# A two-layer transformer trunk on one core: where the weight casts, an activation table and the turned norm stand at the end of the attention heads

## The chip, the core and the metric

The kernel runs on one core of a Trainium2 chip. The metric is the device time of one execution in microseconds (us), the median of several runs; less is better. The core has four engines that matter here, each with its own queue of instructions worked in order: TensorE (PE, matrix products and transposes; PEld is its loading of the stationary operand), VectorE (DVE), ScalarE (ACT) and GpSimd (POOL). SyncE (SP) issues most of the DMAs. All data is float32; products are made in a split form, below.

## The reference

Two layers act on one sequence of 512 tokens with 1024 features. Layer 0 mixes tokens by attention, layer 1 by a gated spatial mixing, and each is followed by a dense MLP. What matters for this change is layer 0:

```python
h = rms_norm(x, norm_mix[i]) * (1.0 + sc1) + sh1
q, k, v = jnp.split(h @ w_in, 3, axis=-1)      # 16 heads of 64; q and k normed
s = q @ k.T + bias                             # per head, causal by chunks of 64
p = softmax(s)
y = (p @ v) @ w_out
x = x + g1 * y
h = rms_norm(x, norm_ffn[i]) * (1.0 + sc2) + sh2
x = x + g2 * (jnp.square(jax.nn.relu(h @ w1)) @ w2)   # w1: 1024 x 4096, w2: 4096 x 1024
```

## The kernel before

Tokens are tiled by 128 (four token tiles t), features by 128 (eight k). A float32 operand is split into a high part, rounded to the type that PE multiplies in one pass, and a low part, the rest. `mm3` makes three products (high x high, high x low, low x high) into one PSUM bank, so a token tile of 1024 features by 512 outputs takes 8 x 3 = 24 matmuls. Splitting a weight tile of 128 x 1024 takes one ScalarE cast (line L388 in `wload`, L485 in `Split`) and one VectorE subtraction (L389, L486). Buffers are 49 slots of one size that are handed out in turn: a new tile waits until the last reader of the slot's former tile is done, and the DMA that fills it waits in SP's queue.

The heads. A loop over heads has four parts in a pipeline: `head_a` (load the bias, turn q and k), `head_b` (scores, the addition of the bias with the row maximum on VectorE at L1218, the exponential on ScalarE at L1223), `head_c` (transposes of the probabilities, L1256, and their split, L1260 and L1261), `head_d` (product with v; then, for each pair of heads, the sums: copy L1284, add L1285, multiply L1293, and the split of the output into `oT` by L1300 and L1301). The output weights' left half is loaded in the loop (`out_load(0)`), and `out_early` makes the products of its first six k as PE has room, one token tile in each of the last turns of the loop.

Behind the loop PE's order is the program's (`in_order`); the order of the other engines, and that of PE inside the loop, is planned ahead of the run by a list scheduler with costs of its own, which takes instructions in the program's priority as soon as it counts them ready. `tc.issue_after(x)` adds the one rule that instructions of its block stay behind x on x's engine. What follows the loop: load x again, `out_load(1)` (right half of the output weights: four loads, four casts, four subtractions), the last `out_early`, the products of k = 6 for all token tiles, those of k = 7 (they need L1300 of the last pair) with the residual added for the left half (L424 multiplies by the gate, L425 adds), and then for each token tile the 24 products of the right half, the residual, and the norm in two steps:

- `norm.rows(t)`: two squares with row sums on ScalarE (L304), then on VectorE and ScalarE the inverse root (`rsqrt_m2`: L130, L131 with the activation Abs_reciprocal_sqrt, L133, L137), then VectorE scales the rows (L306).
- `norm.cols(t)`: PE turns the scaled rows by eight transposes (L315), ScalarE applies scale and shift (L319), VectorE splits (L325, L326).

In the kernel before, `norm.cols(t - 1)` stands behind the products of tile t, and that of the last tile stands in the MLP. `ffn` begins with eight up weights (`up_load` L740, `up_split`), four in each of two groups `ws[0]` and `ws[1]`; its first products take 256 tokens (tiles 0 and 1) at a time: the 96 of group 0, then `norm.cols(3)`, then the 96 of group 1, then the same for tiles 2 and 3. L844 stores x to DRAM.

Of the kernel before, what the change touches and what calls it, by code (L numbers as in the profile page):

```python
# [52 lines left out]
def trunk_kernel(  # L53
# [240 lines left out]
    def split_of(tiles):  # L294
        return [(tiles[k // 2][0][:, k % 2, :], tiles[k // 2][1][:, k % 2, :]) for k in range(2 * len(tiles))]

    normed = [None]

    def norm_rows(t, eng=V):
        nt, ni = SL.get([P, D], F32)  # L300
        ss = st.tile([P, 2], F32, tag="ss", name="ss")
        for hf in range(2):
            sl = slice(hf * 512, hf * 512 + 512)
            A.activation(nt[:, sl], xt[t][:, sl], AF.Square, scale=D ** -0.5, accum_out=ss[:, hf:hf + 1])  # L304
        r = rsqrt_m2(ss[:, 0:1], 1, 1, ss[:, 1:2])
        normed[0] = eng.tensor_scalar(nt, xt[t], r, -0.5, ALU.mult, ALU.mult)  # L306
        return nt, ni
# [441 lines left out]
    def up_ahead(l):  # L749
        return [up_split(up_load(l, 0, n)) for n in range(4)]  # L750

    def ffn(l, norm, rows, cols, after, bgn, lag=1):
        h = norm.h
        hid = {}
        y = Sum()
        xs = dp.tile([NT, P, D], F32, name=f"xs{l}")

        def up_part(w, ps, rng):
            for k in range(KD):
                mm3(ps, w.hi[:, k, :], w.lo[:, k, :], h[k][0][:, rng], h[k][1][:, rng], k == 0, k == KD - 1)  # L760

        def hid_new(b):
            hid[b] = [SL.get([P, 4, 256], F32) for _ in range(2)]

        def square_relu(ps, dsts):
            r = tp.tile([P, 512], F32, tag="tt", name="r")
            A.activation(r, ps, AF.Relu)  # L767
            n = 512 // len(dsts)
            for i, d in enumerate(dsts):
                v = r[:, i * n:i * n + n]  # L770
                if len(d.shape) == 3:
                    v = v.rearrange("p (a b) -> p a b", a=d.shape[1])
                A.activation(d, v, AF.Square)  # L773

        def up_done(b):
            if b == 7:
                norm.free()
            bg(bgn.pop(0) if bgn else 0)

        def up_steps(b):  # L780
            box = {}

            def load(n):
                box[n] = up_load(l, b, n)

            def prep(n):
                box[n] = up_split(box[n])

            def mult(n):
                if n == 0:  # L790
                    hid_new(b)
                w = box.pop(n)
                ps, pi = bank()
                up_part(w, ps, slice(0, 512))
                square_relu(ps, [hid[b][hf][0][:, n, :] for hf in range(2)])
                PS.free(pi)
                w.free()
                if n == 3:
                    up_done(b)

            return [Step(lambda n=n: load(n), lambda n=n: prep(n), nothing, lambda n=n: mult(n)) for n in range(4)]

        def quarters(q):
            return {(i, j): hid[2 * q + j][i] for i in range(2) for j in range(2)}

        def down_steps(q):
            steps = seven(Spent(lambda: quarters(q)), ffn_w2[l][q * 1024:(q + 1) * 1024, :], y)

            def mult_last(f=steps[-1].mult):
                f()  # L810
                bg(bgn.pop(0) if bgn else 0)

            steps[-1].mult = mult_last
            return steps

        ws = {0: ahead.pop("w") if ahead else up_ahead(l)}
        ws[1] = [up_split(up_load(l, 1, n)) for n in range(4)]
        steps = []
        for q in range(3):
            ups, downs = up_steps(2 * q + 2) + up_steps(2 * q + 3), down_steps(q)  # L820
            late = 2 if q == 2 else 1
            for i, u in enumerate(ups):
                steps += [u] + (downs[2 * (i - late):2 * (i - late) + 2] if i >= late else [])
            steps += downs[2 * (8 - late):]
        run = Run(steps, 4, 4)
        for hf in range(2):
            rng = slice(hf * 256, hf * 256 + 256)
            for b in range(2):
                if hf == 0:
                    hid_new(b)  # L830
                for j in range(2):
                    ps, pi = bank()
                    for n in range(2):
                        up_part(ws[b][2 * j + n], ps[:, n * 256:n * 256 + 256], rng)
                    square_relu(ps, [hid[b][hf][0][:, 2 * j:2 * j + 2, :]])
                    PS.free(pi)
                    if hf == 0 and b == 0 and j >= 2 - lag:
                        norm.cols(NT - 2 + j)
                if hf == 1:
                    for w in ws[b]:  # L840
                        w.free()
            if hf == 0:
                for t in range(NT):
                    SP.dma_start(xs[t], xt[t])  # L844
                    SL.free(xid[t])
        any_order()
        up_done(0)
        up_done(1)
        run.go()
        g = gbc[l, 5][0]  # L850
        in_order()
        parts = {b: Split(t, [P, 4, 256]) for b, (t, _) in quarters(3).items()}
        for b in (6, 7):
            SL.free(*[i for _, i in hid[b]])

        def spent(t):
            if t % 2:
                for j in range(2):
                    parts[t // 2, j].free()

        with tc.issue_after(mark[0].ins):
            merge = y.merge(xs, g)
            merge(0)
        project_last(plain(parts), ffn_w2[l][3072:4096, :], g, rows, cols, after, merge, spent)
# [331 lines left out]
        G.memset(b["bias"][0:64, 448:512], NEG)  # L1196
        hs[hd] = b

    rsums, rwide = {}, {}

    def head_b(hd):
        b = hs[hd]
        e = hd % 2
        q, ka, kb, ids = pairs[hd // 2]
        sc, i3 = SL.get([P, 2, 512], F32)
        b["ids"].append(i3)
        pt = {3: sc[:, 0, :], 2: sc[:, 1, 128:512], 0: sc[:, 1, 0:128], 1: b["bias"][:, 512:768]}
        nm = st.tile([P, NT], F32, tag="nm", name="nm")
        sm = st.tile([P, NT], F32, tag="sm", name="sm")
        if e == 0:  # L1210
            rsums[hd // 2] = st.tile([P, NT, 2], F32, tag="rs", name="rs")
        for it in range(NT):
            n = (it + 1) * P
            ps, pi = bank()
            cols = slice(it * P, it * P + P)
            mm(ps[:, 0:n], q[:, e, cols], ka[:, e, 0:n], True, False)
            mm(ps[:, 0:n], q[:, e, cols], kb[:, e, 0:n], False, True)
            V.tensor_tensor_reduce(  # L1218
                out=pt[it], in0=ps[:, 0:n], in1=b["bias"][:, 512 - n:512], scale=-1.0, scalar=-NEG,
                op0=ALU.add, op1=ALU.min, accum_out=nm[:, it:it + 1],  # L1220
            )
            PS.free(pi)
            A.activation(pt[it], pt[it], AF.Exp, bias=nm[:, it:it + 1], scale=-1.0, accum_out=sm[:, it:it + 1])  # L1223
        V.reciprocal(rsums[hd // 2][:, :, e], sm)
        if e == 1:
            SL.free(*ids)
            rb, rbi = rwide[hd // 2] = SL.get([P, 512], F32)
            G.tensor_copy(
                rb.rearrange("p (t e d) -> p t e d", t=NT, e=2),
                rsums.pop(hd // 2).unsqueeze(3).to_broadcast([P, NT, 2, HD]),  # L1230
            )
        b["pt"] = pt
# [34 lines left out]
    def head_d(hd):  # L1267
# [19 lines left out]
        if e == 1:  # L1287
            rp, ri = bank()
            rb, rbi = rwide.pop(pr)
            for t in range(NT):  # L1290
                T.transpose(rp[:, t * P:(t + 1) * P], rb[:, t * P:(t + 1) * P], ident)
            SL.free(rbi)
            V.tensor_tensor(sums[:, 1, :], sums[:, 1, :], rp, ALU.mult)  # L1293
            PS.free(ri)
            if pr % 2 == 0:
                tiles, ids = new_actT(2)
                oT["t"] += tiles
                oT["i"] += ids
            hi, lo = oT["t"][pr // 2]
            A.copy(hi[:, pr % 2, :], sums[:, 1, :])  # L1300
            V.tensor_tensor(lo[:, pr % 2, :], sums[:, 1, :], f32(hi[:, pr % 2, :]), ALU.subtract)  # L1301
            SL.free(si, vi)

# [88 lines left out]
    norm = mid = Norm(0, 3)  # L1392
    in_order()
    load_x()
    out_load(1)
    out_early(NT - 1)
    oTs = split_of(oT["t"])
    for t in range(NT):
# [6 lines left out]
    SL.free(*out_ids[0])  # L1405
    for t in range(NT):
        ps, pi = bank()
        gemm_tok(oTs, out_w[1], t, ps)
        add_residual(t, 512, ps, gbc[0, 2][0])
        PS.free(pi)  # L1410
        norm.rows(t)
        if t > 0:
            norm.cols(t - 1)
    SL.free(*out_ids[1])
    close(0, 2)
    for i, j in oT["i"]:
# [316 lines left out]
                kept.half(0)  # L1733

    lead[0], keep[0] = 2, 36
    ffn(0, mid, gate_rows, norm.cols, lambda: gate_load(0), [3] * 9)
    close(0, 5)
    xs = dp.tile([NT, P, D], F32, name="xsg")
    for t in range(NT):
# [78 lines left out]
```

## Time and profile before

| | |
|---|---|
| median of 3 runs | 1396.56 us (1395.19 to 1397.65) |
| profiled execution | 1395.72 us, its span 1393.7 us |
| PE busy | 1368.2 us (98%) |
| VectorE, ScalarE busy | 985.6 us (71%), 742.5 us (53%) |
| chain that ended last | PE 86%, VectorE 6%, DMA 4%, ScalarE 2% |
| mean granted clock of PE | 0.994 |

The span is what the profile covers; the execution's own time is about 2 us more. Times in the rows count from the span's start. In a timeline a line with xN is N instructions in a row, with the time from the start of the first to the end of the last; in brackets stands how long the engine was idle before it and whose result ended that.

### The profile page before, as it was taken

To read this page: it belongs to the slowest core of one execution; us is meant where nothing else is said; L and a number is where in the kernel's file an instruction comes from. 1 tells how busy PE (TensorE), PEld (TensorE's weight loads), DVE (VectorE), ACT (ScalarE), POOL (GpSimd) and SP (SyncE) were. 2 spreads that over 40 slices of the span, in tenths; PEclk is the share of its full clock that TensorE was granted. 3 is DMA by queue.
4 is the path that set the end of the run, shared out by engine and by line. 5 is a ranking of instruction groups with operands and counts; after the bars stand their busy time and mean duration, and the time that the engine had idled before them with its cause. 6 is when DMAs were issued, how large, how long until landed. Compare 5 with 4: busy or idle time off the path is not lost.

```text
span 1393.7 us, 18907 instructions
## 1 busy us (share of the span) xinstructions
PE 1368.2 (98%) x7130; PEld 1171.2 (84%) x7130; DVE 985.6 (71%) x1430; ACT 742.5 (53%) x1248; POOL 83.4 (6%) x98
## 2 busy tenths in 40 slices
PE   8999999899999999999999999999999999999998
PEld 7899888779888888888888888888889988888887
DVE  5888989675656776577797686778956455665672
ACT  6637667654554545446576654566435455554530
POOL 0000000000101101000000001000000010100100
PEclk8999999999999999999999999999999999999999
DMA  9747576564667875458445748575447366655541
GB/s 373 241 130 212 166 198 177 201 236 128 156 174 199 184 223 120 121 195 305 150 167 170 223 152 245 150 197 192 153 124 254 76 152 191 134 160 135 106 159 53
DMA packets 97483, 246.68 MB, mean 177 GB/s; under 512 B 8680, under 2 KB 10096, under 8 KB 97392
## 3 DMA queue, kind: packets, MB, share of 16 engines
q1 hardware_dynamic: 79536, 205.62, 44.4%
q0 software_dynamic: 16128, 33.56, 14.5%
q10 hardware_dynamic: 1728, 6.29, 1.2%
q8 instruction: 56, 0.92, 0.3%
q14 instruction: 35, 0.29, 0.1%
HBM read 219.23 MB, written 14.68 MB: 168 GB/s over the span
## 4 chain that ended last, share of the span: by engine, by line
PE 86%; DVE 6%; DMA 4%; ACT 2%; issue 1%; SPq 1%; DVEq 0%; ACTq 0%
PE p L92 83%; DMA s<-in_ada_w 1%; DMA s<-in_a_w_in 1%; DMA s<-xsg 1%; PE p L1623 1%; DVE s L979 1%; DMA s<-s 1%; PE p L1256 1%; ACT s L485 1%; SPq L1181 0%; DVE s L425 0%; PE p L315 0%; DMA s<-vd 0%; DVE s L1218 0%; DVE tr L424 0%
## 5 line engine op out<-in xcount | busy, mean ns | idle before, releaser
L92 PE MATMUL p<-s,s 128*128 128x512 f32 (+2 forms) x6496 | 1305.0, 361 | 10.9 <-DVE nm L1218 2.7
L92 PEld LDWEIGHTS p<-s,s 128*128 128x128 f32 x6496 | 1096.4, 189 | 193.7 <-DVE nm L1218 4.5
L486 DVE TENSOR_TENSOR s<-s,s 128x1024 fp32r<-128x1024 f32 x308 | 370.8, 1221 | 216.5 <-ACT s L485 157.9
L485 ACT CAST s<-s 128x1024 fp32r<-128x1024 f32 x308 | 316.9, 1050 | 199.7 <-PE p L92 110.4
L767 ACT ACTIVATE r<-p 128x512 f32<-128x512 f32 x64 | 38.2, 597 | 126.0 <-PE p L92 126.0
L194 DVE SCALAR_TENSOR_TENSOR s<-s,cs,s 128x1024 f32<-128x1024 f32 x70 | 89.6, 1280 | 14.6 <-DMA s<-in_ada_w 14.0
L627 POOL DMA_DIRECT2D s<-in_ffn_w x48 | 58.3, 1215 | 497.8 <-DVE s L486 392.2
L523 DVE TENSOR_TENSOR s<-s,p 128x512 f32<-128x512 f32 x76 | 50.2, 682 | 15.3 <-PE p L92 15.0
L388 ACT CAST s<-s 128x1024 fp32r<-128x1024 f32 x36 | 37.5, 1050 | 39.7 <-DMA s<-in_ffn_w 14.4
L389 DVE TENSOR_TENSOR s<-s,s 128x1024 fp32r<-128x1024 f32 x36 | 43.5, 1221 | 10.7 <-ACT s L388 10.5
L773 ACT ACTIVATE s<-r 128x256 f32<-128x256 f32 (+1 forms) x112 | 44.9, 442 | 1.4
L424 DVE TENSOR_TENSOR tr<-p,s 128x512 f32<-128x512 f32 (+1 forms) x33 | 22.0, 671 | 31.6 <-PE p L92 31.4
L536 DVE TENSOR_TENSOR s<-s,s 128x1024 f32<-128x1024 f32 x28 | 33.6, 1221 | 10.9 <-PE p L92 10.5
L1223 ACT ACTIVATE s<-s,nm 128x128 f32<-128x128 f32 (+3 forms) x64 | 36.0, 563 | 7.4 <-DVE nm L1218 6.0
L630 DVE TENSOR_TENSOR s<-s,s 128x1024 f32<-128x1024 f32 x28 | 33.9, 1220 | 5.6 <-DMA s<-in_b_w_in 5.4
L319 ACT ACTIVATE tt<-p,mod,mod 128x128 f32<-128x128 f32 x64 | 24.0, 462 | 21.1 <-PE p L315 10.4
L304 ACT ACTIVATE s<-s 128x512 f32<-128x512 f32 x24 | 15.3, 637 | 33.9 <-DVE s L425 32.8
L425 DVE TENSOR_TENSOR s<-s,tr 128x512 f32<-128x512 f32 (+1 forms) x33 | 22.2, 674 | 15.0 <-DMA s<-xsg 14.3
L1261 DVE TENSOR_TENSOR s<-p,s 128x512 fp32r<-128x512 f32 (+3 forms) x64 | 29.3, 484 | 4.0 <-ACT s L1260 3.7
L1218 DVE CUSTOM_DVE_ANT_0 s<-p,s 128x128 f32<-128x128 f32 (+3 forms) x64 | 29.6, 484 | 1.8 <-PE p L92 1.6
L1260 ACT CAST s<-p 128x512 fp32r<-128x512 f32 (+3 forms) x64 | 25.1, 425 | 7.5 <-PE p L1256 6.6
L1627 ACT COPY s<-p 128x512 f32<-128x512 f32 x24 | 13.8, 583 | 26.2 <-PE p L1623 26.2
(147 smaller groups left out, 769.5 us busy)
## 6 DMA issues: line engine op xcount, KB each, us to landing
s<-in_ffn_w SPq DMA_DIRECT2D x116, 512.0 KB, 4.2
s<-in_ada_w SPq DMA_DIRECT2D x96, 512.0 KB, 5.8
s<-in_ffn_w POOLq DMA_DIRECT2D x48, 512.0 KB, 5.8
s<-in_b_w_in SPq DMA_DIRECT2D x48, 512.0 KB, 4.7
s<-in_b_w_out SPq DMA_DIRECT2D x24, 512.0 KB, 4.5
s<-in_a_w_in SPq DMA_DIRECT2D x22, 512.0 KB, 4.7
s<-s SPq DMA_DIRECT2D x64, 128.0 KB, 3.5
vd<-s ACTq DMA_DIRECT2D x12, 512.0 KB, 3.8
```

What stands on the lines that cost most here:

```text
L92: T.matmul(ps, lhsT, rhs, start=start, stop=stop, skip_group_check=more)
L194: V.scalar_tensor_tensor(acc, r, ck, acc, ALU.mult, ALU.add)
L388: A.copy(hi, raw)
L389: engs[len(ids) // 2 % len(engs)].tensor_tensor(lo, raw, f32(hi), ALU.subtract)
L485: A.copy(self.hi, raw)
L486: mark[0] = V.tensor_tensor(self.lo, raw, f32(self.hi), ALU.subtract)
L523: V.tensor_tensor(dst, dst, ps, op)
L627: G.dma_start(raw[name, s_][0], block(i, j, s_), accum_op=ALU.add)
L630: V.tensor_tensor(raw[a, s_][0], raw[a, s_][0], raw[b, s_][0], ALU.add)
L767: A.activation(r, ps, AF.Relu)
L773: A.activation(d, v, AF.Square)
L1223: A.activation(pt[it], pt[it], AF.Exp, bias=nm[:, it:it + 1], scale=-1.0, accum_out=sm[:, it:it + 1])
```

## The change

Four edits, all around the end of the heads. The casts of the output weights' right half are kept behind the last exponential on ScalarE. A one-column Abs_reciprocal_sqrt of a constant is put behind the last output cast (L1300), so that the table which the norm needs is loaded there. The casts of the first four up weights are kept behind that same output cast, and those of the next four behind the last square of the norm. The norm's transposes of tile 0 and 1 are put inside the products of tile 2 (after four k) and tile 3 (after three k), and those of tile 2 and 3 behind the first and the second 48 up products (`lag` 2).

```diff
@@ norm_rows
-            A.activation(nt[:, sl], xt[t][:, sl], AF.Square, scale=D ** -0.5, accum_out=ss[:, hf:hf + 1])
+            squared[0] = A.activation(
+                nt[:, sl], xt[t][:, sl], AF.Square, scale=D ** -0.5, accum_out=ss[:, hf:hf + 1]
+            )
@@ ffn
-    def ffn(l, norm, rows, cols, after, bgn, lag=1):
+    def ffn(l, norm, rows, cols, after, bgn, lag=1, first=None):
...
-        ws = {0: ahead.pop("w") if ahead else up_ahead(l)}
-        ws[1] = [up_split(up_load(l, 1, n)) for n in range(4)]
+        with tc.issue_after(first.ins) if first is not None else nullcontext():
+            ws = {0: ahead.pop("w") if ahead else up_ahead(l)}
+        with tc.issue_after(squared[0].ins) if first is not None else nullcontext():
+            ws[1] = [up_split(up_load(l, 1, n)) for n in range(4)]
@@ head_b
-            A.activation(pt[it], pt[it], AF.Exp, bias=nm[:, it:it + 1], scale=-1.0, accum_out=sm[:, it:it + 1])
+            last_of["exp"] = A.activation(pt[it], pt[it], AF.Exp, bias=nm[:, it:it + 1], scale=-1.0, accum_out=sm[:, it:it + 1])
@@ head_d
-            A.copy(hi[:, pr % 2, :], sums[:, 1, :])
+            last_of["o"] = A.copy(hi[:, pr % 2, :], sums[:, 1, :])
@@ behind the heads
-    out_load(1)
+    with tc.issue_after(last_of["exp"].ins):
+        out_load(1)
+    u = st.tile([P, 1], F32, tag="ry1", name="ry")
+    with tc.issue_after(last_of["o"].ins):
+        A.activation(u, f32(ones)[:, 0:1], AF.Abs_reciprocal_sqrt)
...
-        gemm_tok(oTs, out_w[1], t, ps)
+        n = 6 - t if t > 1 else 4
+        gemm_tok(oTs, out_w[1][:n], t, ps, 0, KD - 1)
+        if t > 1:
+            norm.cols(t - 2)
+        gemm_tok(oTs, out_w[1][n:], t, ps, n, KD - 1)
         add_residual(t, 512, ps, gbc[0, 2][0])
         PS.free(pi)
         norm.rows(t)
-        if t > 0:
-            norm.cols(t - 1)
...
-    ffn(0, mid, gate_rows, norm.cols, lambda: gate_load(0), [3] * 9)
+    ffn(0, mid, gate_rows, norm.cols, lambda: gate_load(0), [3] * 9, 2, last_of["o"])
```

## Rows read from the trace of the kernel before

**Rows 1.** Page, busy time, share of the span and instructions of each engine.
```profile
PE 1368.2 (98%) x7130; PEld 1171.2 (84%) x7130; DVE 985.6 (71%) x1430; ACT 742.5 (53%) x1248; POOL 83.4 (6%) x98
```
**Rows 2.** PE's waits, 240 to 310 us: us in total, times, longest.
```profile
PE p L315 <- DVE s L306: 2.4, 2, 1.4
PE p L92 <- ACT s L1300: 2.1, 1, 2.1
PE p L1256 <- ACT s L1223: 1.8, 2, 1.6
PE p L92 <- DVE s L1261: 0.4, 2, 0.3
```
**Rows 3.** Stretches: length, busy time (instructions) per engine, PE's clock, DMA share, GB/s.
```profile
258.00:275.50 17.50, 15.26 (x76) 12.55 (x76) 11.56 (x18) 9.66 (x15) 0.62 (x1) 1.00 0.52 168
...
291.00:306.00 15.00, 13.55 (x72) 11.19 (x71) 12.02 (x31) 8.92 (x25) 0.00 (x0) 1.00 0.45 164
306.00:318.30 12.30, 12.30 (x107) 12.30 (x105) 5.58 (x14) 6.28 (x16) 0.00 (x0) 1.00 1.01 376
...
600.00:784.00 184.00, 184.00 (x833) 152.62 (x832) 138.10 (x148) 111.03 (x198) 4.78 (x6) 1.00 0.61 202
```
**Rows 4.** Timeline of the last exponential, 254 to 258 us.
```profile
253.52 0.68 DVE L1218 CUSTOM_DVE_ANT_0 s<-p,s 128x512 f32<-128x512 f32 x1
...
255.47 1.05 ACT L388 CAST s<-s 128x1024 fp32r<-128x1024 f32 x1 [0.37 <-DMA s<-in_a_w_out]
...
257.06 0.73 ACT L1223 ACTIVATE s<-s,nm 128x512 f32<-128x512 f32 x1
```
**Rows 5.** Timeline of the last pair's output, 270.9 to 277.7 us.
```profile
270.20 1.05 ACT L485 CAST s<-s 128x1024 fp32r<-128x1024 f32 x1 [3.10 <-DMA s<-in_ffn_w]
...
271.27 0.58 ACT L1284 COPY s<-p 64x512 f32<-64x512 f32 x1
271.28 1.23 DVE L486 TENSOR_TENSOR s<-s,s 128x1024 fp32r<-128x1024 f32 x1 [2.23 <-ACT s L485]
...
272.54 0.69 DVE L1285 TENSOR_TENSOR s<-p,s 64x512 f32<-64x512 f32 x1
273.27 0.69 DVE L1293 TENSOR_TENSOR s<-s,p 128x512 f32<-128x512 f32 x1
273.91 1.04 ACT L485 CAST s<-s 128x1024 fp32r<-128x1024 f32 x1 [2.06 <-DMA s<-in_ffn_w]
274.86 0.61 ACT L1300 CAST s<-s 128x512 fp32r<-128x512 f32 x1
```
**Rows 6.** Timeline of the first tile's norm, 286.9 to 291 us.
```profile
286.33 0.69 DVE L425 TENSOR_TENSOR s<-s,tr 128x512 f32<-128x512 f32 x1
...
287.80 1.28 ACT L131 ACT_TABLE_LOAD   x1
...
289.78 0.75 DVE L306 TENSOR_SCALAR s<-s,ru 128x1024 f32<-128x1024 f32 x1
```
**Rows 7.** Timeline of PE alone, 238 to 345 us.
```profile
275.53 14.16 PE L92 MATMUL p<-s,s 128*128 128x512 f32 x60 [2.10 <-ACT s L1300]
...
305.11 1.03 PE L315 MATMUL p<-ident,s 128*128 128x128 f32 x8
305.89 11.76 PE L92 MATMUL p<-s,s 128*128 128x256 f32 x96
```
**Rows 8.** Waits in SP's queue, 225 to 330 us: total, times, longest.
```profile
SPq L844 <- DVE s L425: 15.4, 3, 7.0
```
**Rows 9.** Line L740, the up weights' loads of 250 to 345 us.
```profile
DMA to landing us min/median/max: 3.6/5.4/12.6
```
**Rows 10.** Waits of PE's weight loads, 240 to 310 us: total, times, longest.
```profile
PEld p L92 <- ACT s L1300: 2.5, 1, 2.5
...
PEld p L315 <- DVE s L306: 1.9, 1, 1.9
PEld p L315 <- issue: 1.4, 1, 1.4
```

## What I expect, worked out before the change was run

> **What bounds the kernel now.** I read the busy times first: TensorE (PE) is busy for 1368.2 of 1393.7 us [rows 1], so only about 25 us of the span are PE idle, and a change that issues the same products can win no more than the part of that idle time which it touches. Next I read PE's waits by stretch. From 306 to 784 us the stretches show PE busy for every microsecond (12.30 of 12.30, 184.00 of 184.00, and two between [rows 3]); whatever is won before 306 us should therefore arrive at the end undiminished, unless the change makes a new wait there. The stretch that the diff touches, 258 to 306 us, has holes: 15.26 of 17.50 us busy in its first part, 13.55 of 15.00 in its last [rows 3]. The waits of 240 to 310 us name them [rows 2]: 1.6 us for the last exponential (L1223), 2.1 us for the last output cast (L1300), 2.4 us in two pieces for the scaled rows of the norm (L306), and up to 0.3 us for a subtraction (L1261). The granted clock is 1.00 in all these stretches [rows 3], so no time is to be had from it.
>
> **Output weight casts behind the last exponential.** The scores of the last 512-wide piece leave VectorE at 253.52 + 0.68 = 254.2 us; the exponential starts only at 257.06, because the weight cast of 255.47 (1.05 us, itself waiting 0.37 us for its DMA) and two casts of transposed rows stand ahead of it [rows 4]. Moving four casts away removes the weight cast from that place, and the exponential ends about 1.5 to 2 us sooner, before PE wants it. Gain 1.6 us, and 0.2 us for the subtraction wait behind it that hangs on the same casts; bounds 0 (the casts of transposed rows or a planned order take the place) to 1.9. The weights themselves are wanted only behind the twelve products that start at 275.53 (14.16 / 60 = 0.236 us each [rows 7]), so at 278.4, over 20 us behind the cast of 255.47; this slack hides the move, and without it each cast of 1.05 us would be PE's wait.
>
> **Up weight casts behind the last output cast.** The last pair of heads leaves PE and then runs through ScalarE 0.58, VectorE 0.69 and 0.69, ScalarE 0.61 us before PE may go on. Up weight work stands in between at each step [rows 5]: the copy starts at 271.27 when a cast (270.20 + 1.05) is over, the add starts at 272.54 after a 1.23 us subtraction of weights, and L1300, whose input is ready at 273.27 + 0.69 = 273.96, starts at 274.86 behind the cast of 273.91. Without these three the chain is 0.58 + 0.69 + 0.69 + 0.61 plus three hand-overs of about 0.05 = 2.7 us. PE covers it with the twelve products of the pair before (k = 6), 12 x 0.236 = 2.8 us. Nearly all of the 2.1 us goes; I leave 0.3 for hand-overs. Gain 1.8, bounds 0.9 (L1300's own delay alone, 274.86 - 273.96) to 2.1.
> What comes late instead: four casts (4.2 us) and their subtractions (4.9 us) now fall into the residual adds. Let S be the start of the products after L1300. VectorE then has 0.69 + eight adds of 0.68 + 4 x 1.22 = 11.0 us of work, ready at S + 11.0 where the first half of the second output pass is ready at S + 36 x 0.236 = S + 8.5: 2.5 us of delay for the first norm. That would cost PE in the old order; the next part hides it.
>
> **Norm turned two tiles behind.** From the residual add at 286.33 to the end of the scaled rows at 289.78 + 0.75 takes 4.2 us [rows 6], with one multiply of 0.68 before: 4.9, or 3.6 without the table load. Before, PE wanted those rows at the end of the second tile, S + 60 x 0.236 = S + 14.2; now it wants them twelve products later, S + 17.0. They come at S + 8.5 + 3.6 = S + 12.1, or S + 14.6 with VectorE's delay: at least 2.4 us to spare. The second tile's rows come at S + 14.2 + 3.6 = S + 17.8 and are wanted after eight transposes (0.8 us, 305.11 to 305.89 [rows 7]), twelve and nine products, S + 22.8: 5 us to spare. So both pieces of 2.4 us go; bounds 1.4 (one piece stays) to 2.4. The first up products now follow the second tile's transposes by only 15 products, 3.5 us, and read its eight columns one after the other; if ScalarE and VectorE serve the third tile's residual first, a part of a microsecond is lost there. I take 0.4, bounds 0 to 1.0. The third tile is turned after the first 48 up products; this moves 0.8 us of transposes and costs nothing.
>
> **Table asked for ahead.** The load of 1.28 us stood in the first norm's chain [rows 6]; behind L1300 it stands ahead of four casts that nobody wants for 27 us. With the two-tile distance the norm is no longer PE's wait, so I cost this edit at 0; without that distance it would be worth up to 1.3.
>
> **Second group of up weights behind the last square.** The last token tile ends on PE at S + 22.8 + 0.8 + 3.5 = S + 27.1; add 1.4 and square 0.8 give S + 29.3, four casts S + 33.5, the last subtraction S + 34.7. Their products start after 96 products (11.8 us, [rows 7]) and two sets of transposes at S + 40.5. Cost 0, cover 6 us and more.
>
> **Sum.** 1.6 + 0.2 + 1.8 + 2.4 - 0.4 = 5.6 us. The profiled execution took 1395.72 (span 1393.7 and 2.0 around it), so 1390.1; the median of the three runs stands 0.84 above it, so I forecast 1391.0. With each term's near and far bound the gain is 0 + 0.9 + 1.4 - 1.0 = 1.3 to 1.9 + 2.1 + 2.4 = 6.4. A difference under 0.2%, 2.8 us, can hardly be told from none.
>
> **Rivals.** *The head end gives nothing.* The four output weight casts (4.2 us on ScalarE, 4.9 on VectorE) now lie between the last exponential and the last pair's transposes, each still behind its DMA, and hold up the casts of the last probabilities as they held the exponential; the planned order on PE may shift as well. Then the first two gains stay away and 2.4 us of L306 are left: 1394.1. For it speaks that one weight cast that waited sufficed to cost 1.6 us; against it that PE has two groups of 18 early output products (18 x 0.236 = 4.2 us each) over this place and one full chain less of weights in it. [...]
> *The holes are wider than PE's rows say.* The weight loads have waits of their own in the same places, 2.5, 1.9 and 1.4 us [rows 10], 5.8 together where the products wait 2.1 + 2.4 = 4.5. If this start-up is regained too, the sum before deductions is 6.0 + 1.3 = 7.3 us: 1389.3. Against it: a weight load that waits while products ahead of it still run has lost nothing. [...]
> *Slower: the second group of up weights comes late.* The third and fourth load of that group reuse buffers that PE lets go in the last token tile, and SP works in order behind the stores of x, which held it for up to 7.0 us [rows 8]. Issued behind the last store, at about S + 29.7, and with cast and subtraction (2.3 us) they must have landed by S + 44.0 for the third tile's product at S + 46.3: a flight of 14.3 us. The slowest of before took 12.6 [rows 9], in the stretch where the DMA share was 1.01 [rows 3], and loads that reuse the four raw buffers held longer now join that stretch. From 14.3 us on PE waits; above 19.9 the whole gain is gone. With twice 12.6 PE waits 10.9: 1391.0 + 10.9 = 1401.9.
> *No effect*: the plan for the other engines comes out differently and puts as much idle time elsewhere: 1396.6.
>
> **How the numbers follow.** Forecast 0.63 (own range 1389.6 to 1393.0), wider holes 0.10, head end gives nothing 0.17, no effect 0.05, slower 0.05. Faster by over 0.2%: the first two, 0.73; within: 0.22; slower: 0.05. The range runs from 1388.6, just below the wider holes, to 1395.6, above the head-end rival; outside are the last two rivals and a tail.
>
> **What would show it.** In the profile after: no PE wait of L1256 for the last exponential; the wait for the last output cast at 0.5 us or less, with S near 272; no wait of the norm's transposes (L315 of before) for scaled rows; the table load near 273; the first 256-wide up products near 299 instead of 305.89; PE still busy throughout to 780. It is wrong if transposes of the first tile wait inside the third tile's products, if up products wait for a weight cast, or if the last pair's chain again starts behind weight work.

## The result

The changed kernel ran at a median of 1389.64 us (1387.55 to 1390.47, 4 runs), the kernel before beside it at 1397.11; the ratio is 0.9950, 95% interval 0.9932 to 0.9967, so 4.6 to 9.5 us less. With more runs (the first experiment below) it is 0.9970 (0.9959 to 0.9981), 2.7 to 5.7 us less. The forecast of 1391.0, 5.6 us less, lies in both, in the second just inside its edge. The profiled execution took 1389.62 us, its span is 1387.8.

First the waits of PE, 240 to 320 us (us in total, times, longest). Lines of the changed kernel have moved: L1223 is now L1227, L1261 L1265, L1285 L1289, L1300 L1304, L306 L308, L315 L317, L389 L391.

```profile
PE p L92 <- DVE s L1265: 0.7, 1, 0.7
PE p L1260 <- DVE s L1289: 0.4, 1, 0.4
PE p L1295 <- DVE s L1265: 0.4, 1, 0.4
PE p L92 <- DVE nm L1222: 0.2, 1, 0.2
```

Against [rows 2] the three large waits are gone: none for the exponential, none for the last output cast, none of the transposes for scaled rows. Three new ones stand there, 1.5 us together, for subtractions and an addition on VectorE. PE's own timeline shows where:

```profile
240.33 4.88 PE L92 MATMUL p<-s,s 128*128 128x512 f32 x22 [0.18 <-DVE nm L1222]
...
254.70 4.35 PE L92 MATMUL p<-s,s 128*128 128x512 f32 x18
...
260.14 0.33 PE L1260 MATMUL p<-ident,s 128*128 128x128 f32 x1 [0.44 <-DVE s L1289]
260.82 0.63 PE L1295 MATMUL p<-ident,s 128*128 128x128 f32 x4 [0.35 <-DVE s L1265]
262.20 26.52 PE L92 MATMUL p<-s,s 128*128 128x512 f32 x118 [0.75 <-DVE s L1265]
288.56 1.04 PE L317 MATMUL p<-ident,s 128*128 128x128 f32 x8
...
312.04 33.23 PE L92 MATMUL p<-s,s 128*128 128x256 f32 x275
```

Three marks of this view serve for all that follows: the 22 products ahead of the last exponentials (here 240.33), the long run of products behind the last head's transposes (262.20; before 263.78), and the first product of the second up group (312.04; before 318.28). From the first mark to the second it took 21.9 us before and takes 21.9 us now: the 1.6 us that PE no longer waits for the exponential come back as the three waits. From the second to the third it took 54.5 and takes 49.8. The whole stretch shrank from 76.4 to 71.7, by 4.7 us. Behind it both kernels have the same way to go (1075.4 and 1075.8 us to the end of the span). The rest of the difference of the two spans, 1.5 us, lies ahead of any edit: the 22 products start at 241.85 before and at 240.33 after. A longer fall of PE's clock in the first 40 us (from 15 to 30 us it was 0.65 to 0.69 before, 0.73 to 0.95 after) had set the kernel before back by 1.65 us, but that was made up by 171 us, where the same transposes start at 170.85 and 170.76. The lead comes from a second fall, in before and not in after, between 188 and 194 us (0.50 from 190 to 192 us, where after has 1.00); the stretch (length, busy time of the engines, clock, DMA share, GB/s) of before and of after:

```profile
186.00:194.00 8.00, 6.43 (x29) 5.59 (x30) 8.00 (x24) 5.50 (x14) 0.00 (x0) 0.79 0.72 206
```

```profile
186.00:194.00 8.00, 6.55 (x44) 5.89 (x44) 8.00 (x26) 5.51 (x13) 0.00 (x0) 1.00 0.76 209
```

PE is busy about as long in both, and does 29 instructions in the one and 44 in the other; behind it the lead is 1.9 us (the next transposes start at 193.62 and 191.74).

So of the 5.9 us between the two spans only some 4.4 belong to the change (4.7 won, 0.3 lost behind the stretch).

### The profile page after: what moved, and what is told of

Same layout as the page of the kernel before. It is cut to its first block, busy times and chain, and to the rows that moved or that the text cites. A ratio compares the mean times of both kernels' runs of the same rounds, so it can differ in the third digit from the quotient of the medians.

```text
span 1387.8 us, 18908 instructions
## 1 busy us (share of the span) xinstructions
PE 1365.1 (98%) x7130; PEld 1168.0 (84%) x7130; DVE 985.6 (71%) x1430; ACT 742.3 (53%) x1249; POOL 83.5 (6%) x98
## 3 DMA queue, kind: packets, MB, share of 16 engines
q0 software_dynamic: 16128, 33.56, 14.6%
## 4 chain that ended last, share of the span: by engine, by line
PE 86%; DVE 6%; DMA 4%; issue 2%; ACT 2%; SPq 0%; POOL 0%; DVEq 0%; ACTq 0%; POOLq 0%
PE p L92 83%; DMA s<-in_a_w_in 1%; DMA s<-xsg 1%; DMA s<-in_ada_w 1%; PE p L1633 1%; DVE s L1222 1%; DVE s L1265 0%; PE p L1260 0%; DMA s<-vd 0%; ACT s L487 0%; DMA s<-s 0%; PE p L207 0%; PE p L317 0%; DVE s L427 0%; DVE s L194 0%
## 5 line engine op out<-in xcount | busy, mean ns | idle before, releaser
L391 DVE TENSOR_TENSOR s<-s,s 128x1024 fp32r<-128x1024 f32 x36 | 43.4, 1222 | 10.3 <-ACT s L390 10.1
L426 DVE TENSOR_TENSOR tr<-p,s 128x512 f32<-128x512 f32 (+1 forms) x33 | 22.0, 672 | 31.6 <-PE p L92 31.3
L1227 ACT ACTIVATE s<-s,nm 128x128 f32<-128x128 f32 (+3 forms) x64 | 36.0, 564 | 7.8 <-DVE nm L1222 6.4
L427 DVE TENSOR_TENSOR s<-s,tr 128x512 f32<-128x512 f32 (+1 forms) x33 | 22.1, 675 | 15.0 <-DMA s<-xsg 14.4
L1265 DVE TENSOR_TENSOR s<-p,s 128x512 fp32r<-128x512 f32 (+3 forms) x64 | 29.3, 486 | 2.8 <-ACT s L1264 2.4
L1264 ACT CAST s<-p 128x512 fp32r<-128x512 f32 (+3 forms) x64 | 25.0, 427 | 5.5 <-PE p L1260 4.4
```

The costliest lines, as they stand in the source:

```text
L391: engs[len(ids) // 2 % len(engs)].tensor_tensor(lo, raw, f32(hi), ALU.subtract)
L1227: last_of["exp"] = A.activation(pt[it], pt[it], AF.Exp, bias=nm[:, it:it + 1], scale=-1.0, accum_out=sm[:, it:it + 1])
```

## The experiments

All are compared with the kernel before, run beside them on the same chip. "Stretch" is the time from the first to the third mark in the one profiled execution of each; in the first profile of the changed kernel it was 71.7.

| run | ratio to before (95% interval) | stretch, us |
|---|---|---|
| kernel before | 1 | 76.4 |
| e1 changed kernel | 0.9970 (0.9959 to 0.9981) | 72.5 |
| e2 output casts free | 0.9969 (0.9958 to 0.9979) | 71.8 |
| e3 norm one tile behind | 1.0004 (0.9993 to 1.0014) | 77.1 |
| e4 up casts free | 0.9969 (0.9958 to 0.9981) | 72.6 |
| e5 norm's edit alone | 0.9986 (0.9975 to 0.9998) | 73.7 |
| e6 no early table | 0.9976 (0.9965 to 0.9987) | 74.0 |
| e7 output casts behind the probabilities | 0.9944 (0.9932 to 0.9957) | 69.3 |
| e8 output casts behind the output | 0.9973 (0.9961 to 0.9984) | 73.4 |
| e9 as e7, again | 0.9942 (0.9927 to 0.9957) | 69.3 |
| e10 as e7, up casts free | 0.9988 (0.9978 to 0.9998) | 74.2 |
| e11 as e7, no early table | 0.9954 (0.9939 to 0.9968) | 69.3 |

**e1, the changed kernel.** No edit.

> The changed kernel itself, as the measure for the next runs. Compared is also the stretch on PE from the 22 products ahead of the last exponentials to the first product of the second up group: 318.28 - 241.85 = 76.4 us before, 312.04 - 240.33 = 71.7 in the changed kernel. Theory A (the gain is all in this stretch, 2.1 at the last output cast and 2.4 at the norm, while the 1.8 at the last exponential are given back right behind it): stretch 71.7 within 0.3, time 4 to 5 us below the kernel before. Theory B (a further 2 to 3 us are gained elsewhere, as the medians of 1389.64 and 1397.11 would have it): the same stretch, time 7 us below.

1391.53 us beside 1395.04 before. The ratio gives 4.2 us less and leaves little room for theory B's 7; the stretch came out at 72.5, 0.5 more than theory A's bound, through another 0.24 us wait for a subtraction and small shifts in the heads. The 7.5 us between the first medians were a small sample (4 runs each).

**e2, output casts free.**

```diff
-    with tc.issue_after(last_of["exp"].ins):
-        out_load(1)
+    out_load(1)
```

> The changed kernel without the first edit: the output weight casts are free to stand ahead of the last exponential again. Theory A (edit worth nothing, its four subtractions on VectorE only move the wait to the transposes and products behind): stretch 71.5 to 72.5 us, time within 1 us of the changed kernel; the wait of 1.6 us for the exponential is back and the waits for the subtractions of the last head's probabilities (1.5 us together) are gone. Theory B (edit worth its 1.8 us as forecast): stretch 73.5, time 1.8 us above the changed kernel.

1391.76 us, as e1. PE's waits, 238 to 325 us:

```profile
PE p L1260 <- ACT s L1227: 1.6, 2, 1.3
PE p L92 <- DVE s L1265: 0.7, 3, 0.3
...
PE p L92 <- DVE s L328: 0.2, 1, 0.2
```

The wait for the exponential is back (1.3) and the new waits are gone, apart from small ones that the kernel before has too; the wait for L328 belongs to the norm's edit (the deduction, below). The edit is worth nothing where it was put. VectorE in the changed kernel shows why:

```profile
255.40 2.36 DVE L391 TENSOR_TENSOR s<-s,s 128x1024 fp32r<-128x1024 f32 x2 [0.76 <-ACT s L390]
...
258.14 1.22 DVE L391 TENSOR_TENSOR s<-s,s 128x1024 fp32r<-128x1024 f32 x1
259.39 0.69 DVE L1289 TENSOR_TENSOR s<-p,s 64x512 f32<-64x512 f32 x1
260.12 0.56 DVE L1265 TENSOR_TENSOR s<-p,s 128x384 fp32r<-128x384 f32 x1
260.59 1.22 DVE L391 TENSOR_TENSOR s<-s,s 128x1024 fp32r<-128x1024 f32 x1
261.72 0.42 DVE L1265 TENSOR_TENSOR s<-p,s 128x256 fp32r<-128x256 f32 x1
```

The casts follow the exponential at once, and their four subtractions (L391, 1.2 us each) stand between the short subtractions and the addition for which PE waits: L1289 is wanted by the transposes of 260.14 and L1265 by those of 260.82 and the products of 262.20.

**e3, the norm's transposes one tile behind again.**

```diff
-        n = 6 - t if t > 1 else 4
-        gemm_tok(oTs, out_w[1][:n], t, ps, 0, KD - 1)
-        if t > 1:
-            norm.cols(t - 2)
-        gemm_tok(oTs, out_w[1][n:], t, ps, n, KD - 1)
+        gemm_tok(oTs, out_w[1], t, ps)
...
+        if t > 0:
+            norm.cols(t - 1)
...
-    ffn(0, mid, gate_rows, norm.cols, lambda: gate_load(0), [3] * 9, 2, last_of["o"])
+    ffn(0, mid, gate_rows, norm.cols, lambda: gate_load(0), [3] * 9, 1, last_of["o"])
```

> The changed kernel with the norm's transposes back at one tile behind, as before; the table still asked for ahead, the casts still held back. Theory A (the distance of two tiles is what hides the norm): two waits of the transposes for the scaled rows, 2 to 3.5 us together, time 2 to 3.5 us above the changed kernel. Rival (the early table alone would have taken the first wait away): one wait of about 1.4 us at the second tile, none at the first.

1396.15 us, 4.6 above e1: all of the gain is gone. There is one wait, not two, and at the first tile, not the second, so neither theory had it quite: the early table did not save the first transposes, since the up weights' casts and subtractions now stand in the residual adds. PE's wait and what followed, from the timeline and the stretches:

```profile
290.52 1.75 PE L317 MATMUL p<-ident,s 128*128 128x128 f32 x8 [2.12 <-DVE s L308]
291.92 6.75 PE L92 MATMUL p<-s,s 128*128 128x512 f32 x24
298.51 1.03 PE L317 MATMUL p<-ident,s 128*128 128x128 f32 x8
299.30 5.73 PE L92 MATMUL p<-s,s 128*128 128x512 f32 x24
```

```profile
290.52:292.00 1.48, 1.48 (x9) 1.48 (x9) 0.45 (x1) 1.48 (x3) 0.00 (x0) 0.57 0.15 58
292.00:294.00 2.00, 2.00 (x7) 1.61 (x6) 1.23 (x5) 2.00 (x8) 0.00 (x0) 0.50 0.54 219
```

The hole of 2.1 us is followed by transposes and products at 0.57 and 0.50 of the full clock. Eight transposes take 1.75 us where the next eight take 1.03, 24 products 6.75 where the next 24 take 5.73: another 1.7 us on top of the wait. Another 1.6 us of this profile's stretch are not the edit's: the clock fell as well behind the three short waits near 262 us, which this kernel has in common with the changed one (0.57 between 263 and 267 us). So the edit's own price in the profile is 2.1 + 1.7 = 3.8 us.

**e4, up casts free.** The two `issue_after` in `ffn` taken away.

```diff
-        with tc.issue_after(first.ins) if first is not None else nullcontext():
-            ws = {0: ahead.pop("w") if ahead else up_ahead(l)}
-        with tc.issue_after(squared[0].ins) if first is not None else nullcontext():
-            ws[1] = [up_split(up_load(l, 1, n)) for n in range(4)]
+        ws = {0: ahead.pop("w") if ahead else up_ahead(l)}
+        ws[1] = [up_split(up_load(l, 1, n)) for n in range(4)]
```

> The changed kernel with the up weight casts free. Theory A (these casts and subtractions in the last pair's chain cost the 2.1 us of the last output cast): that wait is back at 1.5 to 2.1 us, time 1.5 to 2.1 us above the changed kernel. Rival (with the heads' order changed PE no longer waits there anyway): wait under 0.5 us, time the same within 0.5.

1391.34 us, the same as e1 in time; in the profile the wait for the last output cast (here L1302) is back at 1.3 us:

```profile
PE p L92 <- ACT s L1302: 1.3, 1, 1.3
```

In time this run does not decide between the two answers: the interval of each ratio is about 1.5 us to either side. In the profile the 1.3 us do not come through whole either: from the second mark to the third it takes 0.9 us longer than in the changed kernel (50.77 and 49.84), since 0.4 us that are lost there further on, at the up products (the deduction, below), are not lost here. e10 asks again.

**e5, the norm's edit alone** on the kernel before.

```diff
-        gemm_tok(oTs, out_w[1], t, ps)
+        n = 6 - t if t > 1 else 4
+        gemm_tok(oTs, out_w[1][:n], t, ps, 0, KD - 1)
+        if t > 1:
+            norm.cols(t - 2)
+        gemm_tok(oTs, out_w[1][n:], t, ps, n, KD - 1)
...
-        if t > 0:
-            norm.cols(t - 1)
...
-    ffn(0, mid, gate_rows, norm.cols, lambda: gate_load(0), [3] * 9)
+    ffn(0, mid, gate_rows, norm.cols, lambda: gate_load(0), [3] * 9, 2)
```

> The kernel before with the norm's edit alone (transposes two tiles behind, lag 2); all casts free, no early table. Theory A (the edits add up: 2.4 at the norm, 2.1 at the last output cast): the two waits for the scaled rows are gone, the waits of 1.6 for the exponential and 2.1 for the output cast stay; stretch on PE from the 22 products to the second up group 74.0 us, time 2.4 us below the kernel before. Rival (the norm's edit carries all of it, since the run with the up casts free was as fast in time as the changed kernel): 4 us below.

1393.32 us; the ratio gives 2.0 us less (0.3 to 3.5), the stretch 73.7 where 74.0 was expected. The transposes no longer wait; the other two waits stay:

```profile
PE p L92 <- ACT s L1300: 2.7, 1, 2.7
PE p L1256 <- ACT s L1223: 1.3, 2, 1.1
```

The edits add up (theory A): 2 to 2.7 us are the norm's.

**e6, no early table.**

```diff
-    u = st.tile([P, 1], F32, tag="ry1", name="ry")
-    with tc.issue_after(last_of["o"].ins):
-        A.activation(u, f32(ones)[:, 0:1], AF.Abs_reciprocal_sqrt)
```

> The changed kernel without the early table: the load of 1.28 us stands again in the first tile's norm. Theory A (the first norm has 2.4 us or more to spare under the distance of two tiles): no wait of the transposes, stretch 71.7 within 0.3, time the same within 0.5. Rival (the early table is what keeps the first transposes on time): a wait of up to 1.3 us at the first transposes.

1392.78 us, 0.6 in a thousand above e1, inside both intervals. The transposes do not wait. The stretch is 74.0 all the same, and the reason that the profile shows is not the table: after the waits near 262 us the clock fell.

```profile
259.00:264.00 5.00, 3.33 (x19) 2.40 (x18) 4.94 (x8) 3.28 (x7) 0.00 (x0) 1.00 0.37 108
264.00:268.00 4.00, 4.00 (x11) 3.12 (x11) 1.74 (x4) 0.62 (x1) 0.00 (x0) 0.57 0.26 49
```

PE was busy for 3.33 of 5.00 us, and then ran eleven products in 4 us, where the same 4 us hold 21 in e1, at a clock of 1.00. The 118 products took 28.17 us where e1's and the changed kernel's took 26.5: 1.6 us. The same waits stand in the profiles of the changed kernel, e1, e3, e4 and e6; in e3 and e6 the clock fell behind them, to 0.57; in the changed kernel and e1 it stayed at 1.00, and e4's 46 products behind them were as fast as e5's without them (9.65 and 9.67 us).

**e7, output casts behind the last head's probabilities.** The first edit with another instruction to stay behind: the last cast of `head_c` (L1264).

```diff
-            A.copy(dst[:, 0, :], src)
+            last_of["p"] = A.copy(dst[:, 0, :], src)
...
-    with tc.issue_after(last_of["exp"].ins):
+    with tc.issue_after(last_of["p"].ins):
         out_load(1)
```

> The changed kernel with the output weight casts held back further, behind the last cast of the last head's probabilities instead of the last exponential. Theory A (the four subtractions ahead of the last probabilities' own caused the 1.5 us of new waits): neither the wait for the exponential nor those for the probabilities' subtractions; from the 22 products to the 46 behind the heads 20.2 us instead of 21.9, time 1.5 us below the changed kernel. Rival (the same work then stands in the last pair's chain): wait for the last output cast 1 us or more, time as the changed kernel.

1387.60 us (1386.05 to 1389.59), the fastest: 7.8 us below the kernel before (6.0 to 9.5). Its waits on PE in 236 to 325 us, and PE's three marks:

```profile
PE p L92 <- DVE s L1265: 0.3, 1, 0.3
PE p L1260 <- ACT s L1227: 0.2, 1, 0.2
PE p L92 <- DVE nm L1222: 0.2, 1, 0.2
```

```profile
239.44 4.86 PE L92 MATMUL p<-s,s 128*128 128x512 f32 x22 [0.20 <-DVE nm L1222]
...
259.10 26.29 PE L92 MATMUL p<-s,s 128*128 128x512 f32 x118
...
308.71 7.55 PE L92 MATMUL p<-s,s 128*128 128x256 f32 x61
```

From the first mark to the second it takes 19.7 us instead of 21.9, 0.5 less than expected. On VectorE the four weight subtractions now stand behind the last L1265, in a place where PE has products queued:

```profile
259.45 0.89 DVE L1265 TENSOR_TENSOR s<-p,s 128x512 fp32r<-128x512 f32 x2 [0.23 <-ACT s L1264]
260.56 4.63 DVE L391 TENSOR_TENSOR s<-s,s 128x1024 fp32r<-128x1024 f32 x4 [0.23 <-ACT s L390]
```

In time the step from e1 is 3.6 us, in the stretch 2.4 to 3.2. That the rest is the clock fits the profiles, since no wait above 0.3 us is left here, but is not shown.

**e8, output casts behind the last output cast.** As e7 with `last_of["o"]`.

> The changed kernel with the output weight casts behind the last output cast, beside the first up weights. Theory A (nothing in the heads needs them): no new wait in the heads, 20.2 us from the 22 products to the 46, and the right half's products, which start 2.8 us after the output cast, just get their first weights (cast 1.05 and subtraction 1.22 us, plus the table's 1.28 if that stands ahead); time 0.5 to 1.5 us below the changed kernel. Rival (the weights come too late): the right half's products wait for casts and subtractions, 1 to 4 us, time 0 to 3 us above the changed kernel.

1392.10 us, as e1. The heads are as quick as in e7 (19.7 us between the first two marks), and the right half's products wait only 0.4 us for a subtraction. What neither theory named: eight casts and eight subtractions now stand in the residual adds, and the first norm is late.

```profile
PE p L317 <- DVE ru L137: 2.0, 1, 2.0
PE p L92 <- DVE s L391: 0.4, 1, 0.4
```

```profile
287.10:289.10 2.00, 0.03 (x1) 0.00 (x0) 1.54 (x7) 0.80 (x4) 0.00 (x0) 1.00 1.01 403
289.10:293.00 3.90, 3.85 (x14) 3.36 (x15) 3.16 (x7) 3.68 (x9) 0.00 (x0) 0.56 0.15 59
```

Here too the clock fell behind a hole of 2.0 us, to 0.56.

**e9, e7 again**, beside the last two.

> The version with the output weight casts behind the last head's probabilities once more, as the measure for the two runs beside it and as a repeat on another occasion. Theory A: 69.3 us within 0.3 on PE from the 22 products to the second up group, time 7 us (5.5 to 8.5) below the kernel before. Rival (its lead over the changed kernel was luck of the occasion): 4 us below.

1387.66 us beside 1396.43; stretch 69.3. The lead is no luck of the occasion.

**e10, e7 with the up casts free** (the diff of e4).

> That version with the up weight casts free. Theory A (they cost the last pair's chain 1 to 2 us on PE, and the equal time of the earlier run with free casts was the resolution of the timing and 0.8 us of other waits in the profile beside it): a wait of 1.2 to 2.7 us for the last output cast, stretch 70.5 to 72, time 1 to 2.5 us above the run beside it. Rival (holding them back is worth nothing, since what is won at the output cast is paid later): time the same within 0.5.

1394.62 us, 6.4 above e9 by the ratios. PE's wait for the last output cast, ScalarE ahead of it, and PE's stretch behind it:

```profile
PE p L92 <- ACT s L1302: 3.6, 1, 3.6
```

```profile
271.81 1.05 ACT L487 CAST s<-s 128x1024 fp32r<-128x1024 f32 x1 [1.74 <-DMA s<-in_ffn_w]
272.76 0.61 ACT L1302 CAST s<-s 128x512 fp32r<-128x512 f32 x1
```

```profile
273.43:277.00 3.57, 3.57 (x9) 2.57 (x10) 3.03 (x4) 3.33 (x4) 0.00 (x0) 0.54 0.85 286
```

On ScalarE the output cast stands behind an up cast that waits 1.74 us for its DMA and takes 1.05. The wait is a microsecond longer than theory A's bound: the heads are done 2 us sooner than in e4, but PE's products go on at 273.43 here and at 273.21 there, since the same weights are waited for. Behind the wait the clock falls, to 0.54: the 72 products that follow take 18.29 us, and in e5 16.88 (16.89 in e4, whose clock is 1.00 from 273.2 to 279 us), so 1.4 us more. Once the heads are free, holding the up casts back is worth more in time than any other edit measured here.

**e11, e7 without the early table** (the diff of e6).

> That version without the early table. Theory A (worth nothing under the distance of two tiles): no wait of the first transposes, time the same within 1 us. Rival (the table's 1.28 us delay the first norm past its 2.4 us to spare): a wait of 0.1 to 1 us at the first transposes and 1 us in time.

1389.05 us, stretch 69.3, no wait of the transposes. The ratio lies 1.2 in a thousand (1.7 us) above e9's, and the intervals overlap; the profile shows no microsecond of it in the stretch. Far behind it this profile loses 3.3 us against e9's between 686 and 825 us, at a wait that the two kernels without the early table show (1.7 us in e6), and of the others e10 alone, at 0.3:

```profile
PE p L92 <- ACT s L1609: 2.0, 1, 2.0
```

A subtraction of weights on VectorE waits for a store to DRAM that sets its buffer free, 2.6 us here, 2.3 in e6 and not at all in e9, and the inverse root of layer 1 stands behind it. Whether that hangs on the missing table or on the spread of the store is open; both profiled executions are the slowest of their kernels. At the place it was made for, the table is worth nothing that can be shown; what it is worth over the whole, 0 to 1.7 us, these runs do not tell.

## Why the prediction was right, and where it was not

**The sum.** 5.6 us forecast, 4.7 in the profiled stretch, 4.2 (2.7 to 5.7) by the larger sample. The first term was not there, the second came out above its size, the third as forecast, and the deduction was paid: 2.1 + 2.4 - 0.4 = 4.1. The other 0.6 us of the 4.7 had no term: the holes gave back somewhat more than PE's waits (below). That the total lies near the forecast is in part luck: a term of 1.8 us was missing, and the first four runs of the changed kernel (7.5 us between the medians) flattered it.

**Output weight casts behind the last exponential: 1.8 forecast, 0 measured.** This is the step that failed. It looked at ScalarE alone, where the weight cast did stand ahead of the exponential. It priced the four subtractions that follow the casts (4.9 us of VectorE) only in the rival that the head end gives nothing, and believed that PE's two groups of 18 products cover them. They cover one, that of 254.70; the other is made behind the loop, in the long run of 262.20, and stands behind the waits. That rival was right about the place for this edit and wrong for the next one. e7 shows that the wait was there to be won, 2.2 us, with the same casts held back behind five casts more.

**Up weight casts behind the last output cast: 1.8 forecast, 2.1 measured.** The chain ran as worked out; on ScalarE of the changed kernel L1304 starts 0.03 us after its input and the up casts follow the table:

```profile
271.15 0.62 ACT L1304 CAST s<-s 128x512 fp32r<-128x512 f32 x1 [1.48 <-DVE s L1297]
271.79 1.28 ACT L1403 ACT_TABLE_LOAD   x1
...
273.19 3.88 ACT L487 CAST s<-s 128x1024 fp32r<-128x1024 f32 x4
```

S, the start of the products behind it, was put near 272; it is 271.8, where L1304 ends (the long run of PE does not break there). No wait is left. e4 and e10 bring it back, at 1.3 and 3.6 us.

**Norm two tiles behind: 2.4 forecast, 2.4 measured, on a thinner cover.** The first tile's rows were worked out for S + 12.1 to 14.6, wanted at S + 17.0. VectorE shows them later:

```profile
286.62 0.68 DVE L426 TENSOR_TENSOR tr<-p,s 128x512 f32<-128x512 f32 x1
287.23 0.74 DVE L308 TENSOR_SCALAR s<-s,ru 128x1024 f32<-128x1024 f32 x1
```

They end at 287.97, S + 16.2, and the transposes start at 288.56: 0.6 us to spare instead of 2.4. The next tile's multiply (L426, whose input PE had just made) was taken ahead of the scaled rows, and the multiply of the tile's second half came at 283.60, S + 11.8, behind the subtractions of up weights. e3 and e8 show what this cover is worth: less distance, or four subtractions more, and PE waits 2 us there.

**The deduction: 0.4 forecast, 0.4 measured,** for up products behind late columns. PE's waits of the changed kernel do not list it, since the gaps are short, but the same 63 products (15 of the last token tile, 48 of the up projection) take longer in the changed kernel than in e5, which has the norm's edit and free casts:

```profile
295.01 9.79 PE L92 MATMUL p<-s,s 128*128 128x512 f32 x63
```

```profile
296.55 9.41 PE L92 MATMUL p<-s,s 128*128 128x512 f32 x63
```

The place is the one that was named: VectorE serves a residual (the last token tile's, L427, where the prediction had the third's) ahead of the last columns of the second tile (L328), and PE's weight loads wait for these.

```profile
299.97 0.69 DVE L427 TENSOR_TENSOR s<-s,tr 128x512 f32<-128x512 f32 x1
300.57 0.42 DVE L328 TENSOR_TENSOR s<-tt,s 128x256 fp32r<-128x256 f32 x1
...
301.05 3.53 PEld L92 LDWEIGHTS p<-s,s 128*128 128x128 f32 x29 [0.32 <-DVE s L328]
```

With the up casts free (e4, e5, e10), and in e8, these products take 9.4 us; in e1, e2, e6, e7, e9 and e11 they take 9.8 or 9.9.

**Early table: 0 forecast, nothing shown at its place** (e6, e11). **Second up group: 0 forecast, 0 measured.** Its four casts start at 301.33, S + 29.5 where S + 29.3 was worked out, and PE wants them at 312.04; the slower rival never came near.

**The wider holes.** From the second mark to the third 54.5 - 49.8 = 4.7 us were won, though 0.4 were newly lost on the late columns; so the holes gave back 5.0 by the exact times. The products' rows promised 2.1 + 2.4 = 4.5, the weight loads' 5.8 [rows 10]: the rival had a part, and the truth lies between. For the size of a hole in this trace the products' rows were the nearer measure, half a microsecond short.

## What to carry to other kernels

An instruction that is held back on one engine drags its followers on another: when a cast is moved, find the place of the subtraction that it feeds, and put both behind the last thing that the bound engine still wants from either queue (e7), but not so late that they fill the next chain (e8). A hole of a microsecond or two on TensorE may cost more than its length: in e3, e6, e8 and e10 the clock fell behind the waits, for another 1.4 to 1.7 us. A list of waits does not show every loss: the 0.4 us of late columns stood only in the length of a run of products, set against the same run in another kernel. And a difference of two medians of four runs each (7.5 us) was over one and a half times what the stretch on PE, cut at marks which both kernels share, had shown at once (4.7).

## What the runs showed of the chip that I had not expected

TensorE's granted clock fell behind some holes inside an otherwise busy stretch, and not behind others. It fell behind waits of 2.0 (e8, to 0.56), 2.1 (e3, to 0.57 and 0.50) and 3.6 us (e10, to 0.54), and behind three waits of 0.58, 0.35 and 0.75 us close together (e6, to 0.57; in e3, with 0.44 for the first, also to 0.57). It stayed at 1.00 behind 2.1 us in the kernel before and behind the three short waits in the changed kernel and e1; the 72 products behind 2.7 us in e5 took no longer than e4's (16.88 and 16.89 us), and the 46 behind the short waits in e4 no longer than those without them in e5 (9.65 and 9.67). Where it fell at the end of the heads, it cost 1.4 to 1.7 us beyond the hole. Ahead of the place of the edits, from 175 to 195 us, its mean was 0.83 to 0.91 in ten of the thirteen profiles; that of the changed kernel is one of the three with 1.00. Each of the falls at the end of the heads stands right behind a hole, but what makes one hole lower the clock and another of about the same length not is open here. It also means that one profile of a kernel with holes may hold such a fall or not: the stretch of e6 is 1.5 us longer than that of e1 by this alone.
